# A hybrid diffusion step: the FFN as three blocks of tokens in float32r and six in float16 pairs, with the attention of two chunks woven through the first

## The chip, the cores and the metric

The kernel runs on one core of a Trainium2 chip. The metric is the device time of one execution in microseconds; the time before is the median of three runs. PE is the matmul engine, DVE, ACT and POOL work on tiles, and SP issues nearly all DMAs.

## The reference

One layer of a diffusion backbone: 128 context tokens (`x_prompt`) and 1024 latent tokens (`x_sample`), all in float32. An input projection feeds eight attention heads and four mLSTM heads (both directions), an output projection merges them, and a SwiGLU FFN follows. Only the parts that the text needs are shown:

```python
def swiglu(h, w_gu, w_down):
    g, u = jnp.split(h @ w_gu, 2, axis=-1)
    return (jax.nn.silu(g) * u) @ w_down

def trunk_layer(x, mods, norm1_w, w_in, ..., rope, ctx_kv, init_f, init_b):
    sh1, sc1, g1, sh2, sc2, g2 = mods
    h = rmsnorm(x, norm1_w) * (1 + sc1) + sh1
    aq, ak, av, mq, mk, mv, mo, mg = jnp.split(h @ w_in, SPLIT_POINTS, axis=-1)
    ...
    attn_o = attention(aq, keys, vals)
    ...
    hm, st_f, st_b = mlstm_bidir(heads(mq), heads(mk) * (MLSTM_DK ** -0.5), heads(mv), gates, init_f, init_b)
    hm = rmsnorm(hm.transpose(0, 2, 1, 3), mlstm_norm_w.reshape(MLSTM_HEADS, MLSTM_DV))
    hm = (hm.reshape(B, T, MLSTM_WIDTH) * jax.nn.sigmoid(mo.astype(F32))).astype(x.dtype)
    mix = jnp.concatenate([attn_o, hm], axis=-1) @ w_out
    x = x + g1 * mix
    h2 = rmsnorm(x, norm2_w) * (1 + sc2) + sh2
    x = x + g2 * swiglu(h2, w_gu, w_down)
    return x, ak, av, st_f, st_b
```

D_MODEL is 1024, D_FF 2816, and 128 rows of tokens are a block: block 0 holds the context tokens, blocks 1 to 8 the latent ones.

## The kernel before, in words

**Precision by pairs.** A float32 operand is split into a high and a low part, and a product is three matmuls: high x high, high x low, low x high. The input projection does this in float16, with scales that are powers of two (`Scaled`, matmuls L487 to L489 and L746 to L748). The FFN and the output projection do it in float32r, which needs no scale: `load_piece` (L138) brings 512 KB of weights into a `raw` tile (two buffers), ACT casts it into `whi` (L151), and POOL, or each third time DVE, subtracts for `wlo` (L134). `whi` and `wlo` have five buffers each.

**Chunks.** Nine blocks are three chunks of three (384 tokens, `CT`). For each chunk, in `GROUPS` of four or five slices of 128 columns of D_FF: `gate_up` (L1337 on) makes 2 x 24 matmuls of 384 columns for each slice (`products`, L1331 to L1335), tanh and two DVE operations, and a high and low part of the activation; `down` (L1369 on) multiplies these with `w_down` in two halves of 512 columns (`three_blocks`, L1152 to L1154), and `add_gated` (L1138) multiplies the result by the gate and adds it to `x1`. All weights of the FFN are so loaded and split three times, once for each chunk.

**What is woven in.** The kernel is written as Python generators: `weave` (L62) advances a side generator by some steps for every unit of the main one, and a list scheduler then fixes each engine's order before the run. In chunk c the attention of chunk c + 1 is woven into the first four groups (50 side steps over 282 units); then `attn_out` (L1240 on, the output projection of that chunk) runs by itself, and `norm2` (L1285 on) beside the last `down`. Chunk 2 has nothing beside its FFN but the `finish` of chunk 1 (final norm and store). `down_last` ends the kernel.

**Attention.** For each block and head: six score matmuls into a three-bank tile `S`, a DVE maximum (L1077), exp on ACT (L1078), a float16 cast (L1081) and the remainder on DVE (L1082), two DMA transposes issued by SP (L1083, L1084), and for each two heads 18 value matmuls (L999). `turned` (L977 on) transposes a block's q into `qT`, which has two buffers.

**Before that.** The input projection for each mLSTM head (`head_project`) has the scan of the head before it woven in (`head_mlstm`, L763 on). The scan multiplies weights for both directions at once (L773), and does its last operations for three blocks at a time (L857 to L867). Then follow q, the attention of chunk 0, and beside it `prefill` (L1189 on): the mLSTM half of the output projection for all nine blocks. For chunks 0 and 1 `x1` stays in SBUF; for the three blocks of chunk 2, x is loaded, added to on POOL and stored (L1231 to L1237).

## Time and profile before

| | |
|---|---|
| median of 3 runs | 1615.27 us (1615.03 to 1615.55) |
| the profiled execution | 1617.88 us |
| its span | 1616.1 us, mean granted clock 0.968 |
| HBM read, written | 178.80 MB, 9.33 MB |
| DMA share, mean | 52.9% of 16 engines |

The page divides the span in 40 slices of 40.4 us; each digit is a busy share in tenths:

```profile
PE   5899999899788868999999999999999999999996
DVE  3944353947787565677753547767764474332445
PEclk8899999999899987999999999999999999999998
DMA  9445353211165664787843546787774445534441
```

The first 2.5 slices are the modulation and the first norm, the next eight the input projection with the mLSTM scans (to some 430 us), then come attention of chunk 0 with `prefill` (to some 640 us), and three stretches of FFN: chunk 0 to some 980 us, chunk 1 to some 1310, chunk 2 to the last matmul near 1603. In the text below "busy time by stretches" is a table with one row for each stretch; "x" in it and in the groups of instructions is a count. A group's row has line, engine, operation, output and inputs, shapes and count, then busy us and mean ns of one, then the idle time just ahead of it and what ended it.

### The profile page before, as it was taken

The page shows a single profiled execution, that of the slowest core. Times are in us where ns is not written, and L with a number is a line of the kernel's source. Part 1 is how long each engine was busy: PE and PEld are TensorE (multiplying, and loading weights), DVE is VectorE, ACT ScalarE, POOL GpSimd, SP SyncE. Part 2 cuts the span into 40 slices and gives each one's busy share as a digit, 9 for nine tenths or more (in the row PEclk, how much of TensorE's full clock was granted, in tenths as well). Part 3 has the DMA queues.
Part 4 walks back from the last instruction along what each step waited for, and adds up shares of the span by engine and source line. Part 5 has one row for each costly group of instructions (what it writes and reads, how often), then busy time and mean ns, then how long its engine had stood idle before and what let it go on. Part 6 is the DMA issues. An engine that isn't in the chain of part 4 may idle for free. (4 is left out here: it accounts for less than half of the span.)

```text
span 1616.1 us, 23209 instructions
## 1 busy us (share of the span) xinstructions
PE 1521.3 (94%) x8688; PEld 1260.8 (78%) x8688; DVE 940.1 (58%) x1821; ACT 730.2 (45%) x1240; POOL 615.8 (38%) x376
## 2 busy tenths in 40 slices
PE   5899999899788868999999999999999999999996
PEld 2655665576557758988999999898898989999995
DVE  3944353947787565677753547767764474332445
ACT  3744343435454455655532344565552443333322
POOL 0411020503247453433345344443344445544443
PEclk8899999999899987999999999999999999999998
DMA  9445353211165664787843546787774445534441
GB/s 344 132 131 144 102 134 73 84 19 32 41 171 119 147 159 100 166 194 169 190 146 118 156 144 208 189 180 165 169 178 124 142 134 174 156 122 147 143 130 66
DMA packets 383270, 227.98 MB, mean 141 GB/s; under 512 B 169174, under 2 KB 345766, under 8 KB 383158
## 3 DMA queue, kind: packets, MB, share of 16 engines
q1 hardware_dynamic: 382598, 225.68, 52.9%
q8 instruction: 68, 1.11, 0.3%
q10 hardware_dynamic: 560, 0.83, 0.1%
q14 instruction: 44, 0.36, 0.1%
HBM read 178.80 MB, written 9.33 MB: 116 GB/s over the span
## 5 line engine op out<-in xcount | busy, mean ns | idle before, releaser
L134 POOL TENSOR_TENSOR wlo<-raw,whi 128x1024 fp32r<-128x1024 f32 x146 | 357.8, 2454 | 450.3 <-ACT whi L151 416.4
L151 ACT CAST whi<-raw 128x1024 fp32r<-128x1024 f32 x219 | 224.3, 1025 | 372.0 <-DMA raw<-in_w_gu_dram 127.8
L1334 PE MATMUL mm<-aTl,whi 128*128 128x384 f32 (+2 forms) x1088 | 366.8, 337 | 0.0
L1335 PE MATMUL mm<-aTh,wlo 128*128 128x384 f32 (+2 forms) x1088 | 366.4, 337 | 0.0
L1333 PE MATMUL mm<-aTh,whi 128*128 128x384 f32 (+2 forms) x1088 | 365.1, 337 | 0.9 <-DVE tn L1361 0.9
L1333 PEld LDWEIGHTS mm<-aTh,whi 128*128 128x128 f32 x1088 | 206.9, 190 | 2.1 <-DVE tn L1361 1.5
L1334 PEld LDWEIGHTS mm<-aTl,whi 128*128 128x128 f32 x1088 | 206.9, 190 | 1.0 <-POOL aTl L134 0.3
L1335 PEld LDWEIGHTS mm<-aTh,wlo 128*128 128x128 f32 x1088 | 207.0, 190 | 0.1
L134 DVE TENSOR_TENSOR wlo<-raw,whi 128x1024 fp32r<-128x1024 f32 (+1 forms) x73 | 88.2, 1208 | 132.9 <-ACT whi L151 132.7
L1152 PE MATMUL mm<-whi,hl 128*128 128x512 f32 x372 | 147.0, 398 | 1.0 <-ACT hl L1365 0.9
L1153 PE MATMUL mm<-wlo,hl 128*128 128x512 f32 x372 | 147.2, 397 | 0.0
L1154 PE MATMUL mm<-whi,hl 128*128 128x512 f32 x372 | 144.4, 397 | 0.7 <-POOL hl L134 0.7
L1082 DVE SCALAR_TENSOR_TENSOR pl<-pr,st,ph 128x1152 f16<-128x1152 f32 x64 | 109.5, 1711 | 46.7 <-ACT ph L1081 46.6
L487 PE MATMUL wi<-ipair,hT 128*128 128x384 f16 (+2 forms) x384 | 124.9, 326 | 2.8 <-ACT ipair L215 2.8
L488 PE MATMUL wi<-ipair,hT 128*128 128x384 f16 (+2 forms) x384 | 124.9, 325 | 0.0
L489 PE MATMUL wi<-ipair,hT 128*128 128x384 f16 (+2 forms) x384 | 124.4, 325 | 0.3 <-POOL hT L134 0.3
L1361 DVE SCALAR_TENSOR_TENSOR tn<-tn,mm 128x384 f32<-128x384 f32 (+2 forms) x68 | 36.7, 540 | 144.4 <-PE mm L1335 110.0
L134 POOL TENSOR_TENSOR hl<-tn,hl 128x384 fp32r<-128x384 f32 x66 | 81.9, 1241 | 96.5 <-ACT hl L1365 90.4
L1142 DVE TENSOR_TENSOR x<-x,t 128x512 f32<-128x512 f32 x102 | 116.1, 1158 | 0.8
L1078 ACT ACTIVATE pr<-S,st 128x1152 f32<-128x1152 f32 x64 | 78.3, 1223 | 80.4 <-DVE st L1077 77.6
L1141 DVE TENSOR_TENSOR t<-mm,gl 128x512 f32<-128x512 f32 x106 | 70.8, 683 | 40.6 <-PE mm L1154 15.8
L1077 DVE TENSOR_REDUCE st<-S 128x1 f32<-128x1152 f32 x64 | 86.5, 1351 | 13.2 <-PE S L1075 12.8
(370 smaller groups left out, 2678.0 us busy)
## 6 DMA issues: line engine op xcount, KB each, us to landing
raw<-in_w_gu_dram SPq DMA_DIRECT2D x132, 512.0 KB
raw<-in_w_down_dram SPq DMA_DIRECT2D x60, 512.0 KB
a<-in_w_ada_dram SPq DMA_DIRECT2D x32, 512.0 KB
gl<-g_d SPq DMA_DIRECT2D x36, 256.0 KB
aw<-in_w_ada_dram SPq DMA_DIRECT2D x16, 512.0 KB
iraw<-in_w_in_dram SPq DMA_DIRECT2D x32, 256.0 KB
raw<-in_w_out_dram SPq DMA_DIRECT2D x15, 512.0 KB
x<-in_x_sample_dram SPq DMA_DIRECT2D x13, 512.0 KB
```

What stands on the lines that cost most here:

```text
L134: (dve if eng == "dve" else pool).tensor_tensor(out=out, in0=full, in1=hi, op=ALU.subtract)
L151: nc.scalar.copy(hi[:, :n], raw[:, :n])
L487: mm(ps[:, :n], ah, wh[:, k % 2, c0 : c0 + n], start=(k == 0), stop=False)
L488: mm(ps[:, :n], ah, wl[:, k % 2, c0 : c0 + n], start=False, stop=False)
L489: mm(ps[:, :n], al, wh[:, k % 2, c0 : c0 + n], start=False, stop=(k == KD - 1))
L1142: eng.tensor_tensor(out=x1[:, cs], in0=x1[:, cs], in1=t, op=ALU.add)
L1152: mm(ps, ah, wh[:, k % 2, :], start=(k == 0), stop=False)
L1153: mm(ps, ah, wl[:, k % 2, :], start=False, stop=False)
L1154: mm(ps, al, wh[:, k % 2, :], start=False, stop=(k == nk - 1))
L1333: mm(ps, wh[:, k, :], th[:, k, :], start=(k == 0), stop=False)
L1334: mm(ps, wh[:, k, :], tl[:, k, :], start=False, stop=False)
L1335: mm(ps, wl[:, k, :], th[:, k, :], start=False, stop=(k == KD - 1))
```

## The change

1. **FFN.** Chunk 0 (blocks 0 to 2) stays in float32r, with `GROUPS` of 4, 4, 4, 4, 3, 3 slices. Blocks 3 to 8 are then done together, in float16 pairs, in groups of 10, 8 and 4 slices (`SIX`): gate and up weights are loaded once for all six. A `Piece` measures its weights on ACT (sum of squares), sums over partitions with a matmul by `ones`, makes a power-of-two scale on DVE and converts. The activations of a group stay float32 until `rescale` finds their common scale.
2. **Down weights.** `split_down` converts `w_down` to scaled float16 pairs once, in three steps for each slice beside gate and up, and stores them in HBM (`wd_d`); `down6` loads them from there, for each half of the six blocks.
3. **Order.** The attention of chunks 1 and 2, the output projection and norm of chunk 1 are woven through the first five groups of chunk 0 (88 side steps over 318 units), those of chunk 2 through the last. All six blocks of `x1` from 3 on go through HBM.
4. **Room for it.** q of blocks 3 to 8 is stored in HBM by POOL and loaded again; q of blocks 1 and 2 is copied by POOL; `qT` has one buffer; `attn_out` takes its operand tile from the tiles `pr` of the softmax.
5. **mLSTM.** The scan's operations are by direction and by block instead of by both directions and by three blocks.
6. `add_gated` in chunk 0's `down` adds on POOL instead of DVE. `bound_h2` makes the scale of the FFN's input.

The diff, cut to its core:

```diff
-GROUPS = [(0, 4), (4, 4), (8, 4), (12, 5), (17, 5)]
-LAST = [(0, 5), (5, 5), (10, 4), (14, 4), (18, 4)]
+GROUPS = [(0, 4), (4, 4), (8, 4), (12, 4), (16, 3), (19, 3)]
+SIX = [(0, 10), (10, 8), (18, 4)]
+SLOTS = 30
...
+                for bb in grp:
+                    if bb >= CB:
+                        pool.dma_start(q_d[bb], q_of[bb])
...
-                wv = wvs[b] = mlp.tile([P, 2, P + 1], F32, name=nm("wv"), tag="wv", bufs=NB)
-                dve.tensor_tensor(out=wv, in0=bc(blocks[b][2], 1, [P, 2, P + 1]), in1=bc(q1[:, :, 4 * b + h], 2, [P, 2, P + 1]), op=ALU.mult)
+                wv = mlp.tile([P, P + 1], F32, name=nm("wv"), tag="wv", bufs=2)
+                dve.tensor_scalar(out=wv, in0=blocks[b][2], scalar1=qcol(1, d, b, h), scalar2=None, op0=ALU.mult)
...
-            dve.tensor_tensor(out=v, in0=v, in1=bc(dn, 3, [P, CB, 2, P]), op=ALU.mult)
-            h3 = hm[:, b0 : b + 1, :]
-            dve.tensor_tensor(out=h3, in0=v[:, :, 0], in1=v[:, :, 1], op=ALU.add)
+            dve.tensor_scalar(out=hm[:, b, :], in0=nu[:, 0, 0:P], scalar1=dn[:, 0:1], scalar2=None, op0=ALU.mult)
+            dve.scalar_tensor_tensor(out=hm[:, b, :], in0=nu[:, 1, 0:P], scalar=dn[:, 1:2], in1=hm[:, b, :], op0=ALU.mult, op1=ALU.add)
...
+    for b in range(1, CB):
+        t = qx.tile([P, NQ * HD], F32, name=f"qx{b}")
+        pool.tensor_copy(t, q_of[b])
+        q_of[b] = t
...
-            qT = ap.tile([P, NQ, P], F32R, name=nm("qT"), tag="qT", bufs=2)
+            qT = ap.tile([P, NQ, P], F32R, name=nm("qT"), tag="qT", bufs=1)
...
-                    if h == 4 and b + 1 in blocks and b + 1 not in qTs:
+                    if h == 4 and c > 0 and b + 1 in blocks:
+                        load_q(b + 1)
+                    if h == NQ - 1 and b + 1 in blocks:
                         qTs[b + 1] = turned(b + 1)
...
-            if gx is None and i != 1:
-                t = ap.tile([P, NQ, P], F32R, name=nm("mx"), tag="qT", bufs=2)
+            if gx is None:
+                t = ap2.tile([P, NQ, P], F32R, name=nm("mx"), tag="pr", bufs=2)
...
+    def split_down():
...
+            raw, v = t[:, 0], wds[:, f, :]
+            act(t[:, 2].bitcast(BF16)[:, 0:1024], raw, AF.Abs, accum_out=v[:, 0:1])
+            powers(v, P)
+            yield
...
+            act(o[:, :, 0], raw, AF.Copy, scale=v[:, 2:3])
+            dve.scalar_tensor_tensor(out=o[:, :, 1], in0=raw, scalar=v[:, 2:3], in1=o[:, :, 0], op0=ALU.mult, op1=ALU.subtract)
+            dma(wd_d[f // 2][:, :, f % 2], o)
+            yield
+
+    class Piece:
...
+        def load(self):
+            self.raw = []
+            for j in range(2):
+                raw = self.own() if self.own else bp.tile([P, 1024], F32, name=nm("braw"), tag="braw", bufs=6)
...
+        def measure(self):
...
+                act(jk, raw, AF.Square, accum_out=v[:, j : j + 1])
+
+        def scales(self):
+            v = self.v
+            ps = bank()
+            mm(ps[:, 0:2], ones, v[:, 0:2], start=True, stop=True)
...
+        def convert(self):
+            self.w = []
+            for j, raw in enumerate(self.raw):
+                t = wp.tile([P, 2, 1024], F16, name=nm("wpair"), tag="whi", bufs=5)
+                sc = self.v[:, 2 + j : 3 + j]
+                act(t[:, 0], raw, AF.Copy, scale=sc)
+                dve.scalar_tensor_tensor(out=t[:, 1], in0=raw, scalar=sc, in1=t[:, 0], op0=ALU.mult, op1=ALU.subtract)
...
+    second = alternate(chain(attn_out(1, one, oT1, gs12), *[norm2(1, one, i) for i in range(CB)]),
+                       attention(2, oT2, set()))
+    main = groups(0, cur, GROUPS[:-1])
+    for _ in range(4):
+        next(main)
+    weave(main, chain(att, second), 18 * 19 - 24, 88)
+    emit(att)
+    emit(second)
...
+    last = chain(attn_out(2, two, oT2, gs2), *[norm2(2, two, i) for i in range(CB)])
+    weave(chain(gate_up(cur, f0, nf), down(0, cur, f0, nf, 0)), last, 15 * nf, 16)
+    emit(last)
+    first = Piece(0, lambda: wp.tile([P, 1024], F32, name=nm("braw"), tag="raw", bufs=2))
+    for i, _ in enumerate(down(0, cur, f0, nf, 1)):
+        if i == 0:
+            first.load()
+        elif i == 1:
+            first.measure()
+        elif i == 2:
+            first.scales()
+        elif i == 3:
+            first.convert()
...
+    def gate_up6(g):
+        for i in range(g["nf"]):
+            f = g["f0"] + i
+            p = pieces[f]
+            for half, (th, tl) in enumerate(h6):
+                pg, pu = bank(), bank()
+                for j, ps in enumerate((pg, pu)):
+                    wh, wl = p.w[j]
+                    products(ps[:, 0:CT], wh, wl, th, tl)
...
+                    if step == 0:
+                        if f + 1 < NF:
+                            if f == 0:
+                                pieces[1].scales()
+                            pieces[f + 1].convert()
+                        if f + 3 < NF:
+                            pieces[f + 3].load()
+                        p.fold()
+                        next(wd_steps, None)
+                    elif step == 1 and f + 2 < NF:
+                        pieces[f + 2].measure()
...
+                    elif step == 3:
+                        if f + 2 < NF:
+                            pieces[f + 2].scales()
...
+    def rescale(g):
...
+        for tn in g["a"]:
+            hl = bp.tile([P, 2, CT], F16, name=nm("hl"), tag="hl", bufs=SLOTS)
+            act(hl[:, 0], tn, AF.Copy, scale=m[:, 1:2])
+            dve.scalar_tensor_tensor(out=hl[:, 1], in0=tn, scalar=m[:, 1:2], in1=hl[:, 0], op0=ALU.mult, op1=ALU.subtract)
...
+    def down_products(ps, g, j, b, w):
+        for k in range(2):
+            hl = g["hl"][2 * (j + k) + b // CB]
+            ah, al = (hl[:, t, b % CB * P : (b % CB + 1) * P] for t in range(2))
+            mm(ps, ah, w[:, k, 0], start=(j + k == 0), stop=False)
+            mm(ps, ah, w[:, k, 1], start=False, stop=False)
+            mm(ps, al, w[:, k, 0], start=False, stop=(j + k == g["nf"] - 1))
```

432 lines of the change are left out of this document (278 added, 154 removed).

## The prediction

> **What bounds the kernel now.** I read the page's first lines, then the busy time by stretches, then the matmuls one by one.
>
> ```profile
> span 1616.1 us, 23209 instructions
> PE 1521.3 (94%) x8688; PEld 1260.8 (78%) x8688; DVE 940.1 (58%) x1821; ACT 730.2 (45%) x1240; POOL 615.8 (38%) x376
> ```
>
> ```profile
> 100.00:430.00 330.00, 312.10 (x2071) 201.03 (x2068) 186.19 (x556) 138.39 (x398) 59.81 (x71) 0.97 0.32 78
> 430.00:640.00 210.00, 175.68 (x890) 134.39 (x891) 139.52 (x249) 104.55 (x152) 107.30 (x65) 0.90 0.59 139
> 640.00:830.00 190.00, 189.53 (x1101) 170.46 (x1101) 129.81 (x177) 104.05 (x137) 73.83 (x36) 0.98 0.75 172
> ...
> 980.00:1020.00 40.00, 38.72 (x211) 36.37 (x211) 22.46 (x37) 17.64 (x25) 18.37 (x10) 1.00 0.65 220
> 1020.00:1220.00 200.00, 197.26 (x1146) 180.60 (x1145) 143.99 (x196) 113.24 (x149) 77.77 (x37) 1.00 0.77 175
> ...
> 1380.00:1604.00 224.00, 223.23 (x1168) 207.36 (x1166) 89.93 (x116) 71.33 (x94) 104.88 (x54) 1.00 0.43 128
> ```
>
> The columns are stretch, length, PE, PEld, DVE, ACT, POOL, granted clock, DMA share, GB/s. From 640 us to the last matmul near 1603 PE hardly ever stands: it is idle 0.5 us while attention of the second chunk is woven in (640 to 830), 1.3 and 2.7 us around that of the third (980 to 1220). So there the time is the number of matmuls times the step from one to the next. Before 640 PE has holes (34 us between 430 and 640), set by chains through DVE, ACT and DMA.
>
> A busy PE says nothing of the step, since matmuls overlap; the timeline does:
>
> ```profile
> 1390.45 0.34 PE L1333 MATMUL mm<-aTh,whi 128*128 128x384 f32 x1
> ...
> 1432.07 0.39 PE L1152 MATMUL mm<-whi,hl 128*128 128x512 f32 x1
> ...
> 1452.97 0.34 PE L1333 MATMUL mm<-aTh,whi 128*128 128x384 f32 x1
> ```
>
> ```profile
> 301.21 0.33 PE L488 MATMUL wi<-ipair,hT 128*128 128x384 f16 x1
> ...
> 308.52 0.33 PE L747 MATMUL wi<-hT,ipair 128*128 128x384 f16 x1
> ```
>
> ```profile
> 443.44 0.38 PE L488 MATMUL mm<-ipair,hT 128*128 128x512 f16 x1
> ...
> 450.13 0.38 PE L489 MATMUL mm<-ipair,hT 128*128 128x512 f16 x1
> ```
>
> Between the first two rows lie 240 gate and up matmuls of float32r, 173.4 ns each; from there 90 of the down projection, 232.2 ns each. The float16 rows of the input projection have the shapes that the changed FFN will have: 45 steps of 384 columns at 162.4 ns, 31 of 512 columns at 215.8 ns.
>
> **The change, part by part.** The sum is made against the profiled execution, 1617.9 us (its span and 1.8 us around it); the median of the runs, 1615.3, lies 2.6 lower, and I take that off at the end.
>
> *Six blocks in float16.* 22 slices x 2 x 8 x 3 = 1056 gate and up matmuls for each 384 tokens, twice: 2112 x (173.4 - 162.4) = **-23.2 us**. Down: 6 blocks x 2 x 22 x 3 = 792 x (232.2 - 215.8) = **-13.0 us**. Both lie on the path, as PE never waits there.
>
> ```profile
> L1333 PEld LDWEIGHTS mm<-aTh,whi 128*128 128x128 f32 x1088 | 206.9, 190 | 2.1 <-DVE tn L1361 1.5
> L487 PEld LDWEIGHTS <-hT 128*128 128x128 f16 x432 | 43.1, 100 | 34.3 <-issue 10.3 <-ACT hT L425 1.2
> ```
>
> A weight load takes 190 ns of float32r, longer than the 173.4 ns step, and 100 ns of float16. The Trainium skill, "TensorE: Matmul & The Clock Gate", section on weight-path perf modes, says that the fast weight load is for 128 weights of a type that is not FP32; the two loads agree. Its section on the back-to-back gap gives N/2.4 + 2.5 ns for a matmul whatever its type, 162.5 and 215.8: the float16 rows agree, the float32r rows are 11 and 16 ns above it, so by that rule alone these two terms would be nothing and the change would gain nothing in the FFN. The rows speak against it, so it gets no chance of its own.
>
> *Small matmuls added.* Each slice gets one matmul with `ones` (2 columns), each of three groups a transpose and one such matmul.
>
> ```profile
> L175 PE MATMUL mm<-pv,one 1*128 1x2 f32 x12 | 2.5, 274 | 2.2 <-DVE pv L164 2.2
> ```
>
> Some 28 of them, between nothing (overlapped) and 0.27 us each, 7.7 us in all. They stand between long matmuls, each with a weight load of its own, so I go nearer the upper end: **+5**. One that waits holds up everything behind it on PE, which is all of the slice.
>
> *Conversions of the six blocks.* Beside a slice's PE time of 96 x 0.1624 = 15.6 us:
>
> ```profile
> L216 DVE SCALAR_TENSOR_TENSOR ipair<-iraw,isc,ipair 128x1024 f16<-128x1024 f32 x8 | 12.4, 1556 | 5.5 <-ACT ipair L215 5.4
> L215 ACT ACTIVATE ipair<-iraw,isc 128x1024 f16<-128x1024 f32 x8 | 9.3, 1162 | 3.6 <-PE wi L489 3.6
> L198 ACT ACTIVATE jk<-iraw 128x1024 bf16<-128x1024 f32 x11 | 11.6, 1057 | 8.1 <-DMA iraw<-in_w_in_dram 8.0
> L1360 ACT ACTIVATE tn<-mm 128x384 f32<-128x384 f32 x64 | 31.0, 485 | 5.5 <-PE mm L1335 5.3
> L1362 DVE TENSOR_TENSOR tn<-tn,mm 128x384 f32<-128x384 f32 x14 | 7.7, 549 | 0.1
> ```
>
> ACT: three measures (two of the gate and up pieces, one of a down row) at 1.06, three casts at 1.16, six operations of 384 columns at 0.49 = 9.6 us. DVE: three remainders at 1.56, six of 384 columns at 0.55, and 13 small ones of at most 0.26 (L857, below), 11.4 us. POOL has almost nothing left. Both engines have 4 to 6 us to spare per slice, and a piece is converted a whole slice ahead. The cost is nothing while that cover holds; I take **+2** for the places where a matmul of `scales` meets a late measure, and for a last stretch in which DVE has the evacuation of six blocks instead of three.
>
> *Second pass of the weights.* 44 pieces less to load, split on ACT and POOL: off the path now (POOL is busy 104.9 of 224 us in the last stretch), so nothing.
>
> *Attention of two chunks in one.* Now 50 side steps lie over 282 units of the main work, in the changed kernel 88 over 318. A unit is 4 matmuls of 173 ns, 0.69 us. A head costs one side step and half of another:
>
> ```profile
> 1195.64 1.05 PE S L1075 x6
> 1196.69 1.87 PE po L999 x17
> ```
>
> ```profile
> L1082 DVE SCALAR_TENSOR_TENSOR pl<-pr,st,ph 128x1152 f16<-128x1152 f32 x64 | 109.5, 1711 | 46.7 <-ACT ph L1081 46.6
> L1077 DVE TENSOR_REDUCE st<-S 128x1 f32<-128x1152 f32 x64 | 86.5, 1351 | 13.2 <-PE S L1075 12.8
> ```
>
> ```profile
> 832.00:872.00 40.00, 40.00 (x232) 40.00 (x232) 11.06 (x14) 13.70 (x19) 21.44 (x11) 1.00 0.44 132
> ```
>
> PE needs 1.05 us for its scores and half of 18 value matmuls, 1.0 us. Now: 1.5 x 282/50 x 0.69 + 2.05 = 7.9 us a head (24 heads in the 200 us from 1020 give 8.3). After: some 43 heads and one output projection (72 x 0.232 = 16.7 us) beside 253 units (70 side steps): 176 + 88 + 17 + norms, about 284 us, **6.6 us a head**. DVE: 144.0/200 x 8.3 = 6.0 us a head now (3.1 of them the two rows above), of which 6.25 us of FFN at 11.06/40 is 1.7; after, 4.3 + 4.1 x 0.277 = 5.4, and the projection's and norms' share, of 6.6. DMA: 0.77 x 8.3 = 6.4 us a head, of which 6.25 x 0.44 = 2.75 is FFN, so 3.65 attention; after 4.1 x 0.44 + 3.65 + 0.3 for output weights and stored x1 and q = 5.75, 87% of 6.6. Both still fit. The projection's four pieces hold four of five weight buffers while gate and up go on with one: then a piece's cast and split stand bare unless side matmuls lie between.
>
> ```profile
> L134 POOL TENSOR_TENSOR wlo<-raw,whi 128x1024 fp32r<-128x1024 f32 x146 | 357.8, 2454 | 450.3 <-ACT whi L151 416.4
> L151 ACT CAST whi<-raw 128x1024 fp32r<-128x1024 f32 x219 | 224.3, 1025 | 372.0 <-DMA raw<-in_w_gu_dram 127.8
> ```
>
>  Bounds: nothing, or 1.03 + 2.45 us for each of some nine pieces, 31 us; the side gives 4 to 6 us of matmuls per piece, so I go near the lower end. Stalls were 4.5 us in the stretches of now; I take 11.5, **+7**.
>
> *First float16 piece.* It can load only when the last down pieces have left `raw`; load, measure, scale and convert are one chain, and 27 matmuls (6.3 us) cover it. Bounds: 0 and a wait as long as this one:
>
> ```profile
> PE mm L113 <- ACT y L1297: 11.2, 3, 7.3
> ```
>
> ```profile
> 600.00:640.00 40.00, 29.73 (x183) 26.66 (x183) 21.06 (x51) 23.07 (x40) 16.50 (x10) 0.85 0.37 86
> 640.00:660.00 20.00, 20.00 (x137) 19.84 (x137) 9.95 (x17) 10.60 (x15) 4.10 (x3) 0.80 0.55 110
> ```
>
> The 7.3 us wait stood at 600 us, and the clock was 0.85 and 0.80 in the 60 us behind it. I take **+3**. The Trainium skill, on the same page, Part 1, has the clock halved after an idle window of about 3.4 us until one busy window has passed: an estimate of 1.7 us more if the wait is that long, which the lowered clock of these rows bears out.
>
> *mLSTM without its batches of three.*
>
> ```profile
> L773 DVE TENSOR_TENSOR wv<-va,QT 128x258 f32<-128x258 f32 x36 | 14.2, 446 | 1.0
> L734 DVE SCALAR_TENSOR_TENSOR so<-so,mwh 128x384 f32<-128x384 f32 x12 | 8.2, 682 | 0.6 <-ACT so L731 0.5
> L862 DVE TENSOR_TENSOR nu<-nu,dn 128x768 f32<-128x768 f32 x12 | 12.1, 1008 | 0.3
> L864 DVE TENSOR_TENSOR hm<-nu 128x384 f32<-128x384 f32 x11 | 9.0, 818 | 0.2
> L802 DVE SCALAR_TENSOR_TENSOR cs<-cs,decb,mm 128x129 f32<-128x129 f32 x56 | 17.1, 346 | 23.5 <-PE mm L792 23.4
> L857 DVE SCALAR_TENSOR_TENSOR dn<-nu 128x6 f32<-128x6 f32 x12 | 3.2, 263 | 0.2
> ```
>
> DVE now, per head: 9 x 0.446 + 3 x (0.682 + 1.008 + 0.818) + 9 x 0.26 = 13.9 us. After, by the nearest row for 128 columns: (16 + 9 + 18) x 0.346 + 27 x 0.26 = 21.9. The 8 us per head lie in a stretch where DVE has 186 of 330 us; only the last scan is bare. Bounds: -2 (no batch stands before the last rescale) and +8; I take **+2**.
>
> *Prefill and q.* Three more blocks of x go through a DMA, a POOL add and a store; six q stores and two copies come to POOL, which is free for 103 of the 210 us from 430. No row shows a DMA issued by POOL; eight jobs at the length of the POOL row above would be 20 us, hidden they are nothing. On SP a store waits for POOL's add, and the transposes of the probabilities queue behind it, on which the value matmuls wait. I take **+2**. One q^T buffer instead of two: the turn waits for the last scores, as the next scores wait for the softmax anyway; in the +7.
>
> Sum: -36.2 + 5 + 2 + 7 + 3 + 2 + 2 = -15.2, 1602.7, and 2.6 lower for the median: **1600 us**.
>
> **Rivals.** *A, the weave is too dense.* If DMA gets no further than its 0.77 of the old attention stretch, a head takes 5.75/0.77 = 7.5 us, 43 x 0.9 = 39 us instead of my 7: **1632, slower**. It decides from 7.1 us a head on. For it: the share I need is above any long stretch's; against it: PE stood only 2.7 us at 0.77.
> *B, all is hidden.* Only the small matmuls are paid: **1584**. For it: nearly no idle PE from 640 on.
> *C, the early stages pay.* mLSTM 8 and prefill 10 instead of 4: **1614, no change**. For it: the holes before 640.
> *D, the conversions bind.* Each slice's `scales` matmul waits 1 us for ACT: 22 us, **1622**. Against it: 9.6 of 15.6 us.
>
> **Numbers.** Forecast (1588 to 1611) 0.54, B 0.20, C 0.08, A 0.12, D 0.06. A change below 0.2% can't be told from none. Faster 0.74, the same 0.08, slower 0.18. Range 1580 to 1626: it takes in B, C, D and the unknown costs' middle, and leaves out A and B's far side.
>
> **What would show it.** Float16 steps of 162 and 216 ns in the FFN; six-block stretch near 520 us with PE idle under 5; heads 6.6 us apart with a DMA share near 0.87; at the switch a wait on the first piece of a few us. Wrong would be PE idle of tens of us in the first chunk, or waits before the `ones` matmul in every slice.

## The result, and the profile after

The changed kernel takes 1653.12 us (median of 4 runs, 1648.07 to 1656.03), the kernel before beside it 1615.15 us. The ratio is 1.0233, with a 95% interval of 1.0203 to 1.0263: slower by 38 us, where 15 us less were forecast, and outside the range. The profiled execution took 1655.72 us. Its page begins:

```profile
span 1654.0 us, 23709 instructions
PE 1506.4 (91%) x8744; PEld 1050.1 (63%) x8744; DVE 974.1 (59%) x2329; ACT 769.0 (46%) x1399; POOL 408.2 (25%) x312
```

PE is busy 15 us less than before, in a span that is 38 us longer. The busy time by stretches of the changed kernel shows where PE stands (columns as before):

```profile
400.00:440.00 40.00, 26.07 (x140) 21.28 (x140) 35.86 (x113) 18.68 (x61) 10.49 (x12) 0.74 0.21 44
660.00:800.00 140.00, 137.72 (x801) 125.81 (x802) 91.33 (x126) 82.11 (x109) 67.70 (x37) 0.96 0.78 174
800.00:822.00 22.00, 15.92 (x88) 13.34 (x87) 12.55 (x20) 12.61 (x19) 5.54 (x4) 0.84 0.78 176
822.00:1020.00 198.00, 193.10 (x1107) 174.87 (x1108) 151.31 (x228) 122.07 (x165) 85.17 (x44) 0.99 0.81 184
1020.00:1060.00 40.00, 33.97 (x158) 28.45 (x157) 16.44 (x23) 9.00 (x12) 18.54 (x12) 0.91 0.48 134
1060.00:1090.00 30.00, 20.36 (x102) 18.68 (x101) 12.24 (x27) 13.49 (x20) 10.04 (x5) 0.86 0.50 158
1090.00:1120.00 30.00, 20.93 (x98) 16.41 (x97) 24.10 (x59) 15.97 (x24) 10.90 (x7) 0.90 0.52 160
1120.00:1300.00 180.00, 179.58 (x1111) 109.04 (x1110) 108.52 (x302) 119.53 (x207) 0.00 (x0) 0.99 0.68 219
1300.00:1640.00 340.00, 340.00 (x1844) 180.36 (x1842) 141.80 (x320) 92.24 (x182) 6.34 (x5) 1.00 0.26 81
```

The float16 part (from 1120 on) is full to the brim. While attention alone is woven in (660 to 800, and most of 822 to 1020) PE is nearly full too, at a DMA share of about 0.8. It stands where the weave changes hands: from 800 on, at the last heads of chunk 1, ahead of its output projection (first matmul at 824.8); and from 1020 on, when attention is over and the projection, the norm and the first float16 piece of chunk 2 follow each other. Before 440, DVE is busy 90% of the last scan and PE 65%.

The matmuls one by one, of the changed kernel's timeline: between the first two rows lie 68 steps, between the others 31.

```profile
1204.71 0.33 PE L1368 MATMUL mm<-h,wpair 128*128 128x384 f16 x1
...
1215.76 0.33 PE L1370 MATMUL mm<-h,wpair 128*128 128x384 f16 x1
...
1555.02 0.38 PE L1677 MATMUL mm<-wd,hl 128*128 128x512 f16 x1
...
1561.71 0.38 PE L1678 MATMUL mm<-wd,hl 128*128 128x512 f16 x1
```

That is 162.5 and 215.8 ns a step; 162.4 and 215.8 were forecast. The view of one tile gives the first and last start of its matmuls; here for the kernel before (values of the scan, mLSTM half of the output projection, gate and up),

```profile
L844 PE MATMUL mm<-va,sd x144: 273/275/533, 177.0 to 421.3; 128*128 128x129 f32 x144
L1184 PE MATMUL mm<-whi,aTh x72: 389/396/632, 473.7 to 562.4; 128*128 128x512 f32 x72
L1333 PE MATMUL mm<-aTh,whi x1088: 221/336/628, 616.6 to 1585.8; 128*128 128x384 f32 x170, 128*128 128x256 f32 x6, 128*128 128x128 f32 x6
```

and here for the changed kernel, with the float16 products last:

```profile
L859 PE MATMUL mm<-va,sd x144: 273/275/582, 190.8 to 437.1; 128*128 128x129 f32 x144
L1216 PE MATMUL mm<-whi,aTh x72: 392/396/774, 491.7 to 599.2; 128*128 128x512 f32 x72
L1368 PE MATMUL mm<-aTh,whi x384: 273/336/686, 643.3 to 1094.2; 128*128 128x384 f32 x160, 128*128 128x256 f32 x16, 128*128 128x128 f32 x16
L1368 PE MATMUL mm<-h,wpair x704: 322/326/528, 1118.3 to 1545.8; 128*128 128x384 f16 x176
```

The scan ends 15.8 us later, `prefill` (from the first to the last start of its 216 matmuls) lasts 108 us instead of 90, and the first gate and up product starts 26.7 us later. To see the rest, I took for each matmul the time to the start of the next, and from it what the same line, type and width usually needs (the 30th percentile); what is left over, summed, is called lost below. From the first gate and up product to the last matmul (1602.8 before, 1639.8 after) that gives:

| us | before | after | difference |
|---|---|---|---|
| up to the first gate/up product | 616.6 | 643.3 | +26.7 |
| matmuls at their usual step | 961.8 | 931.0 | -30.8 |
| lost | 24.3 | 65.5 | +41.2 |

of which 59.6 are lost before the first float16 product. By the same sum 41.7 of these lie where the weave changes hands (10.1 from 800 to 822, 31.6 from 1020 on; the seams, below), and 15.2 in the two woven stretches (7.5 and 7.7; the woven stretches of the kernel before, 640 to 830 and 1020 to 1220, lose 6.2 and 5.7). So the gain is there, and two costs eat it twice over: 27 us early, 41 us in the stretch of chunk 0. What PE waited for there (660 to 1125 us of the changed kernel: total, times, longest):

```profile
PE mm L116 <- ACT y L1330: 11.4, 2, 8.6
PE mm L1368 <- ACT wpair L1536: 7.3, 1, 7.3
PE mm L1368 <- ACT whi L154: 6.4, 4, 3.9
PE po L1025 <- DMA phT<-ph: 3.6, 2, 2.5
PE S L1102 <- DVE qT L137: 3.6, 1, 3.6
```

The first row is the norm (8.6 us of it that of chunk 2), the second the first float16 piece, the third float32r weights; the last two are attention: a wait for the transposed probabilities, and one at 822.7 us for `qT`, which has one buffer now.

### The profile page after: what moved, and what is told of

Its sections match the earlier page's. It is cut to its first block, busy times and chain, and to the rows that moved or that the text cites. A ratio compares the mean times of both kernels' runs of the same rounds, so it can differ in the third digit from the quotient of the medians.

```text
span 1654.0 us, 23709 instructions
## 1 busy us (share of the span) xinstructions
PE 1506.4 (91%) x8744; PEld 1050.1 (63%) x8744; DVE 974.1 (59%) x2329; ACT 769.0 (46%) x1399; POOL 408.2 (25%) x312
## 3 DMA queue, kind: packets, MB, share of 16 engines
q1 hardware_dynamic: 340870, 226.47, 51.3%
## 5 line engine op out<-in xcount | busy, mean ns | idle before, releaser
L1368 PE MATMUL mm<-h,wpair 128*128 128x384 f16 x704 | 230.2, 327 | 7.3 <-ACT wpair L1536 7.3
L1370 PE MATMUL mm<-h,wpair 128*128 128x384 f16 x704 | 230.2, 327 | 0.5 <-DVE wpair L1537 0.5
L1369 PE MATMUL mm<-h,wpair 128*128 128x384 f16 x704 | 230.3, 327 | 0.0
L137 POOL TENSOR_TENSOR wlo<-raw,whi 128x1024 fp32r<-128x1024 f32 (+1 forms) x55 | 136.8, 2488 | 189.6 <-ACT whi L154 184.3
L1109 DVE SCALAR_TENSOR_TENSOR pl<-pr,st,ph 128x1152 f16<-128x1152 f32 x64 | 110.5, 1726 | 47.3 <-ACT ph L1108 47.2
L1744 POOL TENSOR_TENSOR x<-x,fw 128x512 f32<-128x512 f32 x6 | 7.6, 1267 | 521.2 <-ACT jk L1741 521.2
L1368 PE MATMUL mm<-aTh,whi 128*128 128x384 f32 (+2 forms) x384 | 129.6, 339 | 6.4 <-ACT whi L154 6.4
L1369 PE MATMUL mm<-aTl,whi 128*128 128x384 f32 (+2 forms) x384 | 129.3, 337 | 0.2 <-POOL aTl L137 0.2
L1370 PE MATMUL mm<-aTh,wlo 128*128 128x384 f32 (+2 forms) x384 | 129.0, 336 | 0.0
L154 ACT CAST whi<-raw 128x1024 fp32r<-128x1024 f32 (+1 forms) x83 | 84.9, 1026 | 78.9 <-PE mm L1369 26.8
L1368 PEld LDWEIGHTS <-wpair 128*128 128x128 f16 x704 | 70.6, 100 | 51.8 <-ACT wpair L1536 7.3
L1676 PE MATMUL mm<-wd,hl 128*128 128x512 f16 x264 | 100.1, 379 | 0.0
L1677 PE MATMUL mm<-wd,hl 128*128 128x512 f16 x264 | 100.1, 379 | 0.0
L1678 PE MATMUL mm<-wd,hl 128*128 128x512 f16 x264 | 100.1, 379 | 0.0
L1370 PEld LDWEIGHTS <-wpair 128*128 128x128 f16 x704 | 69.0, 98 | 47.0 <-DVE wpair L1537 1.2
L1369 PEld LDWEIGHTS <-wpair 128*128 128x128 f16 x704 | 69.0, 98 | 44.5 <-issue 0.7
L1102 PE MATMUL S<-kst,qT 128*128 128x384 f32 x384 | 84.9, 359 | 10.8 <-ACT pr L1105 7.2
```

The costliest lines, as they stand in the source:

```text
L137: (dve if eng == "dve" else pool).tensor_tensor(out=out, in0=full, in1=hi, op=ALU.subtract)
L1109: dve.scalar_tensor_tensor(out=pl, in0=pr, scalar=st[:, 3:4], in1=ph, op0=ALU.mult, op1=ALU.subtract)
L1368: mm(ps, wh[:, k, :], th[:, k, :], start=(k == 0), stop=False)
L1369: mm(ps, wh[:, k, :], tl[:, k, :], start=False, stop=False)
L1370: mm(ps, wl[:, k, :], th[:, k, :], start=False, stop=(k == KD - 1))
L1676: mm(ps, ah, w[:, k, 0], start=(j + k == 0), stop=False)
```

## The experiments

Each ratio is to the kernel before, measured beside it on the same chip. The times in the second table are read from each run's trace as in the rows above.

| run | ratio | interval |
|---|---|---|
| changed kernel | 1.0233 | 1.0203 to 1.0263 |
| e1, before, mLSTM unbatched | 1.0006 | 0.9986 to 1.0026 |
| e2, changed, mLSTM batched | 1.0154 | 1.0130 to 1.0179 |
| e3, changed, last part early | 1.0467 | 1.0442 to 1.0492 |
| e4, before, dense weave | 1.0034 | 1.0012 to 1.0056 |
| e5, changed, half weights | 1.0354 | 1.0326 to 1.0382 |
| e6, changed, norm not raised | 1.0373 | 1.0346 to 1.0400 |
| e7, before, x1 through HBM | 1.0032 | 1.0014 to 1.0049 |
| e8, changed, five edits | 1.0268 | 1.0248 to 1.0287 |
| e9, as e6, order pinned | 1.0226 | 1.0203 to 1.0248 |
| e10, changed, tail in line | 1.0225 | 1.0193 to 1.0258 |
| e11, e10 and mLSTM batched | 1.0131 | 1.0094 to 1.0167 |
| e12, before, three early parts | 1.0108 | 1.0078 to 1.0137 |
| e13, changed, x1 in SBUF | 1.0127 | 1.0100 to 1.0154 |
| e14, before, q through HBM | 1.0031 | 1.0016 to 1.0045 |
| e15, e10 with 19 slices | 1.0140 | 1.0112 to 1.0169 |
| e16, all mended | 1.0011 | 0.9992 to 1.0030 |
| e17, e16, norm earlier | 1.0007 | 0.9992 to 1.0022 |
| e18, e17 with 20 slices | 0.9988 | 0.9972 to 1.0005 |

| us | scan ends | prefill | prefill to gate/up | gate/up starts | lost to first float16 | lost after it |
|---|---|---|---|---|---|---|
| before | 421.3 | 89.8 | 53.1 | 616.6 | | |
| changed | 437.1 | 108.0 | 43.6 | 643.3 | 59.6 | 5.9 |
| e1 | 432.8 | 88.0 | 52.7 | 620.2 | | |
| e2 | 418.4 | 107.7 | 43.1 | 628.1 | 60.1 | 5.7 |
| e3 | 441.6 | 108.7 | 43.2 | 648.1 | 76.7 | 23.0 |
| e5 | 430.6 | 107.5 | 42.4 | 633.8 | 57.2 | 29.5 |
| e6 | 433.2 | 107.8 | 43.2 | 638.0 | 58.0 | 25.2 |
| e7 | 414.9 | 104.0 | 45.8 | 615.8 | | |
| e9 | 434.0 | 110.6 | 43.2 | 641.0 | 55.6 | 5.7 |
| e10 | 433.2 | 108.8 | 42.6 | 639.4 | 50.2 | 10.6 |
| e12 | 423.5 | 107.7 | 43.2 | 628.4 | | |
| e13 | 435.7 | 89.0 | 51.3 | 629.6 | 55.3 | 5.7 |
| e14 | 420.3 | 94.0 | 49.9 | 619.3 | | |
| e15 | 435.1 | 107.9 | 43.0 | 639.4 | 38.5 | 16.0 |
| e16 | 415.1 | 99.7 | 47.3 | 620.6 | 40.1 | 5.3 |
| e17 | 421.5 | 99.6 | 47.4 | 627.6 | 43.9 | 4.8 |
| e18 | 418.9 | 100.8 | 47.3 | 626.5 | 34.8 | 8.8 |

One profile stands for a median only roughly: e16, e17 and e18 are the same up to chunk 0, and their scans end at 415.1, 421.5 and 418.9 us.

### The mLSTM, alone and undone

e1 puts the changed `head_project` and `head_mlstm` into the kernel before; e2 puts the old ones back into the changed kernel.

> The kernel before, with the mLSTM part of the change alone (weights by direction, the last operations by block). Theory: the last scan runs without cover and DVE sets its pace, so the q stage starts some 16 us later: 1628 to 1635 us. Rival (my prediction's term): DVE has room, 1615 to 1620 us, and the late q stage of the changed kernel has another cause.

> The changed kernel with the mLSTM part of before put back (one tile moved to a later pool to make room, eight weight buffers instead of nine). Theory: last scan matmul near 422 us instead of 437, and the whole 14 to 20 us faster than the changed kernel, 1633 to 1640. Rival: prefill and the first attention are bound by something else, less than 5 us come back.

The same edit costs nothing measurable in one kernel (1 us, give or take 3) and 13 us in the other (1.0233 - 1.0154, by 1615; give or take 6). e1 met its rival; e2 fell just short of its theory. In e1 the scan ends 11.5 us later than before, but the first gate and up product only 3.6 us: most of the room (5.7 us) lies between the scan's end and the start of `prefill`, 46.7 us instead of 52.4. In the changed kernel, undoing the edit brings the scan's end forward by 18.7 us and the first gate and up product by 15.2. So the scan moves less in the one, and more of the move is taken up there; why, these runs don't show.

### The weave: a denser plan before, an earlier projection after

```diff
-            weave(main, chain(previous(c, cur), att), 18 * sum(nf for _, nf in GROUPS[:NG]) - 24, 50)
+            weave(main, chain(previous(c, cur), att), 18 * sum(nf for _, nf in GROUPS[:NG]) - 24, 78)
```

> The kernel before with attention woven in at 78 side steps over 282 units instead of 50, the density of the changed kernel (0.277 a unit). Rival A of the prediction (a dense weave is bound by DMA or DVE): 24 heads twice over cost some 0.9 us more each, 1640 to 1660. Theory: the weave holds this density, 1611 to 1620.

It costs 0.34%, 5 us, but it does not test density. The score matmuls of chunk 2's 24 heads, in the kernel before and then in e4 (1000 to 1200 us):

```profile
L1075 PE MATMUL S<-kst,qT x144: 332/336/444, 1006.1 to 1196.4; 128*128 128x384 f32 x144
L1075 PE MATMUL S<-kst,qT x144: 333/336/445, 1009.0 to 1197.0; 128*128 128x384 f32 x144
```

That is some 8.2 us a head in both, where the edit asked for one in about 5.8 (1.5 x 282/78 x 0.69 + 2.05, by the prediction's own formula). The DMA share is 0.77 from 1020 to 1220 in the kernel before and 0.78 in e4. The heads kept the old pace, so a denser attention was never run and rival A is not cleared by e4. What speaks against it is the changed kernel itself, whose woven stretches lose only 15.2 us.

e3 put the last chunk's projection and norm (`third`) behind the second attention in the main weave:

```diff
-    weave(main, chain(att, second), 18 * 19 - 24, 88)
+    side = chain(att, second, third())
+    weave(main, side, 18 * 19 - 24, 88)
```

> The changed kernel with the output projection and norm of the last chunk woven behind the second attention into the first five groups, so that the last group of three slices runs alone behind it. Theory: the 25 us of idle PE between 1020 and 1118 us come from the end of that side work, which has nothing left to run beside it; 15 to 22 us come back, 1631 to 1638, with a wait of at most 8 us on the first float16 piece left. Rival: the four held weight buffers set it, so the stall moves along with the projection, and under 6 us come back.

It was the other way: 38 us slower than the changed kernel (1.0467 - 1.0233). Of that, 17 us are lost before the first float16 product, and 17 after it, in code that the edit doesn't touch. The next three runs bear on the second 17.

### Weight buffers, the norm's place, and an order that nobody wrote

e5 takes w_out by halves of its columns for chunks 1 and 2, in a function of its own; e6 emits their norm without raised priority.

```diff
+        for n in range(2):
+            ws = out_pieces(0, ns=(n,))
+            for i in range(CB):
...
-            with hot(800):
+            with hot(800 if c == 0 else 0):
```

> The changed kernel with one edit: the output projections of the second and third chunk go through w_out one half of its columns at a time (two weight pieces held instead of four of the five buffers), and each block's attention result is split into its two float32r parts twice. Theory (the four held weight buffers starve the gate/up stream): of the 25 us that PE loses in 800-880 and 1020-1060 us of the changed kernel some 12 to 15 come back, so 1637 to 1644 us against 1653. Rival (PE waits there for attention's transposed DMAs and for the norm, and weights are only queued behind them): nothing comes back, 1650 to 1656, and the extra splits cost 1 to 2.

> The changed kernel with one edit: the norm of the second and third chunk is emitted without raised priority, so its transposes stand in TensorE's order where the program has them and not ahead of gate/up products. Theory (the 8.8 us gap at 1077.8 us, where TensorE stands at a transpose while the sums of squares and the reciprocal root run, is order and not lack of work): 6 to 9 us come back, 1644 to 1648. Rival: the gate/up products were not ready either, and the norm now ends later, so the first float16 products wait longer: 1653 to 1660.

Both theories fell: the loss before the first float16 product shrank by 2 us only, and both kernels were some 20 us slower than the changed one. All of that lies in the six-block stretch (lost: 29.5 and 25.2 instead of 5.9). The waits of ScalarE and PE between 1125 and 1300 us, first of the changed kernel,

```profile
ACT wdt L1487 <- DMA wdt<-in_w_down_dram: 23.2, 10, 7.1
```

then of e6:

```profile
ACT wdt L1487 <- DMA wdt<-in_w_down_dram: 40.8, 11, 7.1
...
PE mm L1368 <- ACT wpair L1536: 5.9, 5, 1.7
PE mm L1370 <- DVE wpair L1537: 4.3, 5, 1.0
```

L1487 measures a piece of `w_down` for a later slice; L1536 converts gate and up weights that PE needs next. Both stand in ScalarE's one queue, and in e6 ScalarE waits 41 us there for loads, with conversions behind it. The list scheduler (the planner of the expectations) had set them so. Pieces measured ahead of the conversions of slice 4, 6, 8 and 10 (counted from one), in the order of ScalarE's instructions:

```
changed kernel   7  11  15  19
e6               7  12  17  22
program order    3   5   7   9   (e9, below, runs in it)
```

The Trainium skill, "TensorE: Matmul & The Clock Gate", section "Architectural detail", says that ScalarE's queue is a strict first-in-first-out one; these rows agree (while ScalarE waits 41 us for loads in e6, PE waits 5.9 us for conversions behind them). e9 is e6 with one line more:

```diff
-            act(t[:, 2].bitcast(BF16)[:, 0:1024], raw, AF.Abs, accum_out=v[:, 0:1])
+            tc.keep_in_program_order(act(t[:, 2].bitcast(BF16)[:, 0:1024], raw, AF.Abs, accum_out=v[:, 0:1]))
```

> The kernel of the experiment with the norm at normal priority, with one line more: the statistics of each w_down piece on ScalarE (L1487) are held to program order, so that the planner cannot put them ahead of conversions that TensorE needs sooner. In that experiment, and in the one with half weights, the stretch of six blocks took 541 and 545 us against 523, with ScalarE waiting 41 us for w_down loads against 23, although no edit touched that stretch; the order of ScalarE's instructions there had changed. Theory (the order that the planner wrote is the cause): the six-block stretch returns to 520 to 526 us and the time to 1645 to 1655. Rival (this chip's transfers are slower, or the stretch wavers from run to run): the stretch stays at 535 to 545, 1660 to 1672.

Its ScalarE wait in the same stretch:

```profile
ACT wdt L1487 <- DMA wdt<-in_w_down_dram: 1.9, 1, 1.9
```

The 24 us are gone (1.0373 to 1.0226), and the six-block stretch takes 521.2 us instead of 540.7. What remains, 1.0226, is the changed kernel's own time, so the norm's priority is worth nothing: in e9 PE still stands 8.6 us before the transposes, as in the changed kernel. e3 has the same shift (40.5 us of that wait), so its theory was worth 17 us of harm in chunk 0, and the 17 after it probably came from the order; e3 was not run with the order held. e8 joined five edits while the order was free, and lost 18 us in the six-block stretch; it can't be read as a sum.

> The changed kernel with all of it: mLSTM as before (11 us alone), half weights, the norm at normal priority, the first float16 piece loaded and measured before the last third of chunk 0's down (its gap was 7.5 us), and prefill's stores on POOL's queue instead of SP's. If the effects add, 1653 - 11 - 13 - 7 - 6 - 4 = about 1612, so level with or a little below before (1605 to 1620). If they have one cause in common, or one gap takes another's place, 1625 to 1640.

### The early parts, one by one and together

e7 puts x1 of blocks 3 to 5 through HBM in the kernel before, e14 q; e12 does all three early parts; e13 takes x1 back into SBUF in the changed kernel (its core is shown; e7 is the reverse).

```diff
-                    if c == 0:
-                        add_gated(x1[i], ps, g, n, pool)
+                    if c < 2:
+                        add_gated(x1s[c][i], ps, g, n, pool)
```

> The kernel before with one edit: in prefill blocks 3 to 5 also go through x1_d as the changed kernel has it (their x rows loaded into a work buffer by halves, added there on POOL, stored, and loaded back after prefill), in place of an add onto rows that lie in SBUF. Theory (this is what makes prefill of the changed kernel 18 us longer: the work buffers and the stores that wait in SP's queue for POOL): prefill 8 to 16 us longer than 90, and 4 to 12 us on the whole, 1619 to 1627. Rival (q through HBM and one qT buffer do it): prefill within 3 us of 90, total 1614 to 1618.

> The kernel before with all three of the changed kernel's early parts: mLSTM unbatched (alone 0.06% slower), x1 of blocks 3 to 5 through HBM in prefill (alone 0.3%, 5 us), and q of blocks 3 to 8 through HBM with one qT buffer. Theory (each alone is partly swallowed by slack between the scan's end and the first gate/up, which the others use up): first gate/up starts 22 to 28 us later than before's 616.6, as in the changed kernel, and the time is 20 to 28 us above before. Rival (they do not add up; the rest of the changed kernel delays its first gate/up in another way): 6 to 12 us above before.

> The kernel before with only q of blocks 3 to 8 through HBM, one qT buffer instead of two and the first q rows copied on POOL. Theory (each of the three early parts costs, and they add: 19 us together, 1 for the mLSTM and 5 for x1 alone): 8 to 14 us above before. Rival (they cost together because each takes the slack that hides the other): 0 to 4 us above before.

> The changed kernel with one part undone: x1 of blocks 3 to 5 is added up in SBUF during prefill, as before, and not sent through HBM (and the w_down statistics in program order, which alone should not change the time). Theory (this part costs in prefill what it cost in the kernel before, where it made prefill 14 us longer and the whole 5 us slower, and nothing later swallows it): prefill back from 108 to 93 to 97 us, the time 1636 to 1644 against 1649 to 1653. Rival (the attention that runs beside prefill ends last anyway): prefill shorter, the first gate/up not earlier, 1647 to 1653.

x1 through HBM costs 5 us in the kernel before and 16 in the changed one (1.0226 for e9 less 1.0127; by the intervals some 10 to 22). The profiles show the same order: 7 us more from the start of `prefill` to the first gate and up product in e7, 11 less in e13.

| from the start of `prefill` to gate/up | us | matmuls in `prefill` | matmuls behind it |
|---|---|---|---|
| before | 142.8 | 405 | 177 |
| e7, x1 | 149.8 | 458 | 124 |
| e14, q | 143.9 | 430 | 148 |
| e12, all three | 150.9 | 472 | 106 |
| changed | 151.6 | 472 | 106 |
| e13, changed, x1 in SBUF | 140.3 | 430 | 148 |

The column "prefill to gate/up" falls from 53 us to 43, and it is tempting to read it as slack that the early parts use up. The counts say otherwise: in the changed kernel 71 fewer matmuls stand behind `prefill` and 67 more within it; the value matmuls of attention behind it go from 53 to none. The longer `prefill` is in part work done earlier, and only the sum of both columns is a delay. In that sum the parts add up: x1 and q alone take 7.0 and 1.1 us, and e12, with both and the mLSTM, 8.1. On the clock, three parts that cost 0.06, 0.32 and 0.31% alone cost 1.08% together; the intervals (their upper ends add up to 1.2%) leave it open whether that is more than their sum. e12 lies between its theory and its rival (its first gate and up product is 11.8 us late, in a profile whose scan ends only 2.2 us late), and so does e14.

So it is shown that the mLSTM and x1 cost more in the changed kernel than in the kernel before (13 against 1, 16 against 5). That they share one slack is not shown.

What in `prefill` takes longer is not settled. Stretches of `prefill`, of the changed kernel and of e13:

```profile
492.00:600.00 108.00, 93.00 (x473) 74.25 (x472) 75.47 (x125) 49.47 (x66) 58.31 (x39) 0.92 0.80 189
```

```profile
489.00:578.00 89.00, 80.18 (x428) 64.32 (x429) 63.66 (x111) 42.82 (x57) 58.62 (x38) 1.00 0.80 175
```

It is not the DMA share, 0.80 in both. SP's waits of its stores for POOL (8.5 us in the changed kernel, 3.9 in e13) fit, but in e8, where the stores went through POOL's own queue, `prefill` took 110 us. The three `t2` buffers, which hold x, the products and the mLSTM rows, are left; that wasn't tried. Nor is x1 the whole of it: in e16 to e18 it is in SBUF too, and `prefill` takes 100 us, with 454 matmuls in it.

```profile
SPq L1269 <- POOL t L1268: 8.5, 7, 2.7
```

```profile
SPq L1269 <- POOL t L1268: 3.9, 3, 3.2
```

### The tail of chunk 0 in line

e10 weaves attention alone through 17 slices; then come both projections with one load of w_out, the last five slices, and the norms in the two `down` halves; the first float16 piece is loaded early, and the order is pinned. e11 adds the batched mLSTM. e15 weaves through 19 slices and keeps three for the tail.

```diff
-    weave(main, chain(att, second), 18 * 19 - 24, 88)
+    side = chain(att, attention(2, oT2, set()))
+    weave(main, side, 18 * f0 - 24, 80)
+    emit(side)
...
+    ws = out_pieces(0)
+    first.load()
...
+    first.measure()
+    emit(gate_up(cur, f0, nf))
...
+        weave(down(0, cur, f0, nf, n), n2, 3 * nf, 8)
```

> The changed kernel with the tail of chunk 0 built as the kernel before has its boundaries: only the attention of chunks 1 and 2 is woven through the first 17 slices; then both output projections in line, with one load of w_out for both; then the last five gate/up slices, which cover the norm's sums and root; the norms woven into the two down halves; the first float16 piece loaded and measured early; w_down statistics in program order. Theory (TensorE loses some 54 us between 660 and 1118 us because projection, norm and first piece stand in the weave with nothing long enough behind them to cover their chains): the loss falls to 15 to 25, so 1613 to 1628. Rival (the loss is the density of the weave, DMA and VectorE together): attention is as dense as before, so most of it stays, 1640 to 1655.

> The same as the experiment with the tail in line, and the mLSTM batched as before (11 us alone). If the effects add: 1602 to 1617, level with or a little faster than before. If the tail's loss stays: 1629 to 1644.

> The experiment with the tail in line, but attention woven through 19 slices with three left for the tail, in place of 17 and five. There 11 heads stood alone behind the last woven slice, and TensorE lost 29 us at 940 to 1003 us. Theory (heads come one by one, each held by its own chain, so what counts is that gate/up lasts as long as they do): the 29 us shrink to below 10, the three slices (25 us) still cover the norm's chain, and the time is 1622 to 1632. Rival (whatever is left without a cover costs the same, now behind the projections): 1640 to 1650.

e10 gave nothing back on the clock; its loss moved. Its stretches,

```profile
680.00:940.00 260.00, 257.81 (x1506) 234.55 (x1505) 170.11 (x239) 154.42 (x202) 130.37 (x69) 1.00 0.80 183
940.00:1003.00 63.00, 41.65 (x205) 31.68 (x204) 41.99 (x60) 30.80 (x39) 12.44 (x7) 0.86 0.91 194
1003.00:1080.00 77.00, 77.00 (x401) 70.62 (x400) 38.53 (x74) 33.61 (x51) 26.46 (x15) 1.00 0.36 117
```

and the one of e15 that answers to the middle row:

```profile
980.00:1006.00 26.00, 15.62 (x76) 11.59 (x75) 17.02 (x24) 12.77 (x15) 14.75 (x9) 0.80 0.93 227
```

The projections and the last slices, in line, run without a hole. But the value matmuls of ten heads stood alone behind the last woven product at 950 us (e15's expectation says eleven), and PE is idle 21 us in these 63; with 19 slices the value matmuls of four heads are left and 10 us. e15 is 15 us faster than the changed kernel (1.0233 to 1.0140), 7 us short of what its theory said. Of its 16.0 us lost after the first float16 product, 13 lie in the first 25 us, where PE waits 5.7 us at a `scales` matmul for ScalarE's measure (3.6 in e10, 4.1 in e18): there the wait for the first pieces came back. e11 met its rival; it is 15 us faster than e10 (1.0225 to 1.0131), which shows the price of the mLSTM a second time.

So the loss is neither the buffers (e5) nor the norm's priority (e9): it belongs to whatever chain is left with no long matmuls beside it, and e15 shows it going down where such matmuls are put. From 940 to 1003 us of e10, where the heads run with hardly a long matmul beside them, the DMA share is 0.91, so the 0.8 of the woven stretches is not the most that was reached.

### All mended

e16 has the batched mLSTM, x1 in SBUF, e15's tail (with 100 side steps asked for instead of 88) and the pinned order. e17 moves the norm of chunk 1 into the last slices, e18 weaves through 20 slices.

> All that helped at once: mLSTM batched, x1 of blocks 3 to 5 in SBUF, the tail in line behind 19 woven slices, w_down statistics in program order. If the single effects add (1649 less 11, less 8, less 20 if the tail's theory holds): about 1610, level with before or just faster; if the tail's rival holds, 1628 to 1635.

> The version with all parts mended, with the norm of chunk 1 woven into the last three gate/up slices and that of chunk 2 into the first down half, so that the second half (6 us of products) stands behind them; before, both norms stood in the down halves, VectorE ran without a break from 1062 to 1078 us and TensorE waited 8.4 us for the first float16 products. Theory (that wait is VectorE's queue of norm work): 6 to 8 us less, so 0.994 to 0.998 of before. Rival (the wait moves into the down halves): no change, 1.000 to 1.003.

> The same with attention woven through 20 slices and two left for the tail. Theory (the 15 us that TensorE still loses at 960 to 985 us are heads alone behind the woven slices): another 4 to 8 us less, 0.989 to 0.996 of before. Rival (two slices, 17 us, are too short to cover the norms): what the heads give back the norms take, 0.995 to 1.002.

e16 is 36 us faster than the changed kernel; the single effects (13, 16 and 15) add up to 44. e17 and e18 met their rivals. e16 is level with the kernel before, and so are e17 and e18. e17's wait for the first float16 products fell from 8.4 to 2.4 us in its profile, but the same sum is lost elsewhere (43.9 instead of 40.1). e18 loses least, 34.8 us, and its ratio, 0.9988, is the best of all, but its interval takes in 1. No version was found that beats the kernel before for certain. In e18's profile the last matmul starts at 1601.0 us, 1.8 before that of the kernel before: the usual steps give 30.8, the extra loss takes 19.3 (34.8 + 8.8 - 24.3) and the later first gate and up product 9.9 (626.5 - 616.6).

## Why the prediction was wrong, step by step

- **Six blocks in float16, -36.2.** Right: 162.5 and 215.8 ns. With the small matmuls (+5) the forecast was -31.2; the usual steps sum to -30.8.
- **Conversions, +2, and rival D.** Right in size: PE waits 0.4 us on a `scales` matmul between 1125 and 1300 us. But "nothing while that cover holds" hid that the cover hangs on an order: e5 and e6 show 20 us when the list scheduler shifts it.
- **Attention, +7 (0 to 31).** This is the step that failed most. The sums over DMA and DVE let heads come 6.6 us apart; they came 8.2 apart (264 score matmuls are 44 heads, from 661.1 to 1014.0 us), about as in the kernel before, and what sets that pace stays open,

```profile
L1102 PE MATMUL S<-kst,qT x264: 333/336/669, 661.1 to 1014.0; 128*128 128x384 f32 x132
```

  yet PE was nearly full beside them, and the pace was not what was paid. The price was put on weight pieces; e5 shows that they are not it. The chains at the seams (projection, norm, heads left over) had no term. Lost: 59.6 us up to the first float16 product, 41.7 of them at the seams, where "tens of us in the first chunk" was named as what would prove the forecast wrong.
- **First float16 piece, +3 (0 to 7.3).** The wait was 7.3 us, the upper end.
- **mLSTM, +2 (-2 to +8).** The DVE work was priced well. The rows after:

```profile
L800 DVE TENSOR_SCALAR wv<-va,QT 128x129 f32<-128x129 f32 x64 | 24.9, 394 | 29.2 <-PE mm L809 29.0
...
L873 DVE SCALAR_TENSOR_TENSOR hm<-nu,dn,hm 128x128 f32<-128x128 f32 x36 | 13.7, 380 | 0.6
L872 DVE TENSOR_SCALAR hm<-nu,dn 128x128 f32<-128x128 f32 x36 | 12.7, 353 | 0.6
L758 DVE SCALAR_TENSOR_TENSOR so<-th,mwh 128x128 f32<-128x128 f32 x36 | 11.4, 318 | 10.7 <-POOL hm L876 9.5 <-ACT th L756 0.8 <-POOL va L754 0.3
```

  These are 62.7 us, 15.7 a head (14.9 by the forecast's 43 operations at 0.346), where the batched rows had 43.5 in all (14.2 + 8.2 + 12.1 + 9.0). But the term was judged by the kernel before, where it indeed costs nothing (e1); in the changed kernel it costs 13 us (e2).
- **Prefill and q, +2 (0 to 20).** x1 alone costs 16 us in the changed kernel (e13). The mechanism named, a store on SP behind POOL's add, is not borne out by e8.
- **The rivals.** A came nearest in time, and heads did come slower than its 7.1 us; but its bill, PE standing in the weave for want of DMA, was not what was paid: the woven stretches were nearly full. A denser weave remains untested. C was right in kind: the early stages pay, 26.7 us instead of its 18. B and D fell. None of them had two costs at once.
- **How the numbers were joined.** With every unknown cost at its upper end the sum is -36.2 + 5 + 2 + 31 + 7.3 + 8 + 20 = +37.1 us, 1652.4 at the median, and 1653.1 was measured. That the two meet is luck: the 31 us were counted for weight pieces, which are not the cause. The error was to take each cost in the lower half of its bounds, by covers that were read from the kernel before. Where the same part was measured in both kernels, it cost 1 and 5 us there and 13 and 16 in the changed one.

## What to carry to other kernels

A part that costs nothing alone tells little of its price in company: measure it in the changed kernel too, by taking it out. Check that an experiment did what was asked before reading it: e4's denser plan left the heads as far apart as they were. And when a stage grows longer, count what runs in it, since part of its length may be work that has moved in from the next. In these runs the weave gave back where long matmuls outlasted the chain beside them, so look at the seams, where one side stream ends and the next begins, and keep independent matmuls for those places. And where a scheduler writes the engines' order from its own estimates, compare the orders before reading an experiment: here an edit moved 20 us in code 100 us away, and one line took them back.

## What the runs showed of the hardware

After an idle time PE starts slowly. In the changed kernel's timeline, behind the wait for the norm of chunk 2:

```profile
1077.75 0.40 PE L1218 MATMUL mm<-whi,mx 128*128 128x512 f32 x1
1086.79 1.11 PE L116 MATMUL mm<-ident,y 128*128 128x128 f32 x4 [8.64 <-ACT y L1330]
...
1088.34 0.52 PE L1370 MATMUL mm<-aTh,wlo 128*128 128x384 f32 x1
1088.66 0.52 PE L1368 MATMUL mm<-aTh,whi 128*128 128x384 f32 x1
...
1092.30 0.34 PE L1368 MATMUL mm<-aTh,whi 128*128 128x384 f32 x1
1092.47 0.34 PE L1369 MATMUL mm<-aTl,whi 128*128 128x384 f32 x1
```

The step is 320 ns until 1091.9 us, then 173: some 13 products at 147 ns more, 2 us on top of the 8.6 us wait. The prediction's estimate from the Trainium skill's page ("TensorE: Matmul & The Clock Gate", Part 1) was 1.7 us for a wait that long; this trace comes near it, with a slow time of 5.1 us (1086.8 to 1091.9) instead of the 3.4 us behind that estimate.
